# Convolution inputs and attention queries turned by way of DRAM, and the second half's groups dealt out anew, in a one-core hybrid block

## The chip, the cores and the metric

The kernel runs on one core of a Trainium2 chip. The metric is the device time of one launch in microseconds (us). One core has TensorE for matmuls (in the profile PE, and PEld for its weight loads), VectorE (DVE), ScalarE (ACT), GpSimd (POOL) and SyncE (SP), and 16 DMA engines that move data between the core's memory and DRAM. Matmul results go to PSUM, which here is cut into banks of 512 columns; all other tiles lie in SBUF.

## The reference

One layer of a streaming encoder on 256 tokens of 2048 features, all in float32:

```python
h = rms_norm(x, mix_norm)
proj = h @ w_in            # q|k|v|z|beta|alpha, mla_q|c_kv|k_rope, gate_a|gate_b
qkv = silu(causal_conv(concat([dn_q, dn_k, dn_v]), conv_w))     # 4 taps per channel
q_a, k_a = l2norm(q), l2norm(k);  o_a = gated_delta_rule(q_a, k_a, v_a, g, beta)   # 8 heads of 128
o_a = rms_norm(o_a) * silu(dn_z)
qn, qr = rms_norm(mla_q[:128]), rope(rms_norm(mla_q[128:]))     # 8 heads of 128 + 64
kn, v_b from rms_norm(c_kv) @ w_kv_up;  o_b = softmax attention, chunk-causal
y = sigmoid(gate_a) * (o_a @ w_branch_a) + sigmoid(gate_b) * (o_b @ w_branch_b)
x = x + y @ w_out
x = x + relu(rms_norm(x) @ w_mlp_up)^2 @ w_mlp_down
x = x + sigmoid(rms_norm(x) @ w_ple_gate) * (p @ w_ple)
```

The gated delta rule needs, per head and chunk, the inverse of a triangular matrix built from k, beta and the decays g, and then two recurrent steps.

## The kernel before

**Main stream.** All large matrix products run as one stream of *groups* (`stream`, from L411 on). A group is 512 (sometimes 464, 384 or 256) output columns of one product for all 256 tokens, accumulated in two PSUM banks over its rows of weights. It is cut into *steps* of 256 weight rows. In a step, `load` brings the weights from DRAM on SP's queue (tile `raw`, five buffers), `cut` splits them into a rounded high part `whi` on ACT and a remainder `wlo` on DVE (helper `split`, L260, recorded under L146; four buffers each, three steps ahead), and TensorE makes 12 matmuls: two rows of 128, two token blocks, and three products (high by high, high by low, low by high) at L501. Left operands are kept likewise as two parts, in `Acts` objects: `hT` (normed input), `cT` (the compressed latent), `obT` and `oaT` (outputs of the two branches), `yT`, `nT`, `uT`, `gT`.

**Groups' order.** The list `groups` gives it: first the small columns, the latent (`ckv`) and the queries of the attention (four groups `evac_mq` of two heads each, 384 columns, the first one inside the first group), with `kv0` to `kv3` (two steps each) among them; then six groups of convolution inputs, k, q, v of the first half of the heads and k, q, v of the second half (`evac_conv`); then four pairs of a gate group `gb` and a branch group on `obT` (`evac_bb`, four steps); then z, `ga`, the branch groups on `oaT`, and the rest. A step of kv, conv and gb groups takes the same 12 matmuls of 512 columns. Counting steps from zero, the first conv group begins at step 48, and the first `obT` group at step 104.

**Side work.** What lies between the products is written as generators that sit in four *lanes*: `L_MLA` (attention), `L_CONV`, `L_SOLVE` (delta rule) and `L_TURN`. After each step the planner `weave` is called twice; each call is one *tick* and runs one piece (up to the next `yield`) of one lane, at most every second tick for a lane. A lane runs its generators one after the other. A generator that waits yields False and costs no turn. Before a matmul of the main stream is written, `until` looks whether its left operand has been written by then; if not, it runs lanes without the gap, tick after tick, until it has. So the order in the program is settled when the program is built; a list scheduler then orders instructions on each engine by program order and by when it expects their inputs, so that an instruction whose inputs are late can be overtaken by later ones. ACT and DVE instructions that go through `keep_in_program_order` stay behind the one written before them on their engine.

**Transposes before.** The conv inputs come with tokens on partitions and must have channels there. `conv` does eight 128x128 transposes on TensorE (L895) into two PSUM banks, and ACT (first tap) and DVE (three taps) read the banks. After the SiLU, eight more TensorE transposes (L918) make token-major copies for norms, k and v. `evac_mq` norms and rotates the queries of two heads, transposes them on TensorE (L731 for the 128 plain, L732 for the 64 rotated features), and ACT and DVE bring the results to `qnT` and `qrT`.

**The way by DRAM that is there already.** Class `Carry` turns `oaT`, `yT`, `nT` and `gT`: DVE transposes 32x32 blocks (`turn`, L324), POOL's queue writes the tile to DRAM (L326) and fetches it back in four loads, one for 32 partitions each (L331); the pieces are read in the lane `L_TURN` 15 ticks after the fetch was written (`CARRY`).

**Gates' values.** `gates` makes the cumulated decays of 16 heads and token blocks (`gmid`, 128 partitions by 16) and writes them to DRAM transposed, element by element (L873); `decays` (L1257) reads them back as rows spread over all partitions.

**Delta rule.** `solve` waits until all four attention parts are done (`mla["ob"]`) and q, k and v of its half, then runs `inverse` and `recur`; the branch `oaT` needs both halves.

**Buffers.** `big` tiles (4 KB a partition) share 23 buffers, `mid` tiles (2 KB) 16; side work has four PSUM banks (`bank`), the main stream four (`acc`).

Of the kernel before, what the change touches and what calls it, by code (L numbers as in the profile page):

```python
# [9 lines left out]
F32 = mybir.dt.float32  # L10
# [7 lines left out]
P = 128  # L18
T = 256
# [133 lines left out]
def hybrid_block(ctx: ExitStack, tc: tile.TileContext, a, dbg=None):  # L153
# [14 lines left out]
    RAW_BUFS, SPLIT_BUFS, AHEAD, BIG_BUFS, EARLY, CARRY = 5, 4, 3, 23, 8, 15  # L168
# [146 lines left out]
    class Carry:  # L315
        def __init__(self, acts, k0):
            self.acts, self.k0, self.name = acts, k0, f"{acts.name}{k0}_"
            self.sq = big(f"sq_{self.name}", shape=(P, NT, 4, P))
            self.there = dpool.tile([NT, P, 4, P], F32, tag="there_sq", name=f"out_{self.name}")

        def turn(self, tb, src):

            tc.keep_in_program_order(
                nc.vector.transpose(self.sq[:, tb].rearrange("p j (k c) -> p k j c", k=4),  # L324
                                    src.rearrange("p (k j c) -> p k j c", k=4, j=4)))
            nc.gpsimd.dma_start(self.there[tb], self.sq[:, tb])  # L326

        def fetch(self, scales=None):
# [4 lines left out]
            return self.landed(land, scales, clock[0] + CARRY)  # L333
# [368 lines left out]

    def evac_mq(g, ps):
# [4 lines left out]
        def work():  # L708
# [19 lines left out]
            tn, tr = bank(f"tp_qn{g}"), bank(f"tp_qr{g}")  # L728
            for tb in range(NT):
                for e in range(2):  # L730
                    pe.transpose(tn[:, e * T + tb * P : e * T + (tb + 1) * P], q[:, tb, e, 0:HD], ident)  # L731
                    pe.transpose(tr[:ROPE, e * T + tb * P : e * T + (tb + 1) * P], rot[:, tb, e, :], ident)  # L732
            mla["qn"][g] = mid(f"qnT{g}")
            act.activation(mla["qn"][g], tn, AF.Copy, scale=gain("q_nope_norm"))
            mla["qr"][g] = mid(f"qrT{g}")
            nc.gpsimd.memset(mla["qr"][g][ROPE:, :], 0.0)
            dve.tensor_copy(mla["qr"][g][:ROPE, :], tr[:ROPE, :])
            yield
# [5 lines left out]
    def evac_kv(g, ps):  # L744
# [9 lines left out]
        def work():  # L754
# [16 lines left out]
            while not mla["kr"]:  # L771
                yield False
# [58 lines left out]
    gmid = cpool.tile([P, NT, NH], F32, name="gmid")  # L831
# [4 lines left out]
    def gates():  # L836
# [35 lines left out]
        with nc.allow_non_contiguous_dma(reason="small"):  # L872
            nc.gpsimd.dma_start(gmid_there.rearrange("b h p -> p b h"), gmid)  # L873
# [6 lines left out]
    def evac_conv(kind, half, ps):  # L880
# [3 lines left out]
        L_CONV.add(conv(kind, half, ev))  # L884

    def conv(kind, half, ev):

        yield
        acc = big(f"cv{kind}{half}", shape=(P, 4, T))
        for pair in range(2):  # L890
            tp = bank(f"tp_cv{kind}{half}{pair}").rearrange("p (h t) -> p h t", h=2)
            for e in range(2):
                for tb in range(NT):
                    h = 2 * pair + e
                    pe.transpose(tp[:, e, tb * P : (tb + 1) * P], ev[:, tb, h * P : (h + 1) * P], ident)  # L895
            for e in range(2):
                h = 2 * pair + e
                ct = "qkv".index(kind) * 8 + half * 4 + h
                w = lambda s: convw[:, (3 - s) * 24 + ct : (3 - s) * 24 + ct + 1]
                act.activation(acc[:, h, :], tp[:, e, :], AF.Copy, scale=w(0))  # L900
                for s in (1, 2, 3):
                    dve.scalar_tensor_tensor(acc[:, h, s:], tp[:, e, : T - s], w(s), acc[:, h, s:],
                                                   ALU.mult, ALU.add)
        yield
        y = acc
# [6 lines left out]
        if kind in "kv":  # L912
            tm = big(f"tm{kind}{half}", shape=(P, NT, 4, HD))
# [508 lines left out]
```

## Time and profile before

| | |
|---|---|
| time, median of three runs | 1529.3 us (1529.29 to 1529.53) |
| the profiled execution's own time | 1529.25 us |
| its span, first to last instruction | 1527.5 us |
| TensorE (PE) busy | 1517.3 us, 99% |
| VectorE (DVE) busy | 997.7 us, 65% |
| ScalarE (ACT) busy | 772.3 us, 51% |
| GpSimd (POOL) busy | 75.3 us, 5% |
| DMA, mean | 198 GB/s |

A row of the *timeline* has start, duration, engine, line, operation, written tile and read tiles, how many are merged, and in brackets the idle time ahead of it with what ended it. A row of one *tile's* view has shortest, median and longest duration in ns, the first and last start in us and the forms. A row of *windows* has the length of a stretch, busy time and number of instructions of PE, PEld, DVE, ACT and POOL, the granted clock, DMA share and GB/s. A row of *DMA issues* has the count, the size of each and the median time from issue to landing. The durations of matmuls overlap, since they are pipelined: their price is the distance of their starts.

### The profile page before, as it was taken

Reading aid. Unit: us, or ns where it says so; the run is one execution under the profiler, and the core shown is the slowest. Engines: PE = TensorE matmul, PEld = TensorE weight load, DVE = VectorE, ACT = ScalarE, POOL = GpSimd, SP = SyncE. Lnnn points to the kernel's source line nnn. Section 1 sums busy time; section 2 is a strip of 40 time slices with the busy share of each in tenths; the row PEclk is TensorE's granted clock in tenths of the full one; section 3 lists DMA queues with packets and bytes.
Section 4 is the critical chain, followed back from the end, with each engine's and each line's share of the span. In section 5 each row is a group of like instructions: output and inputs, shape, how many; then the busy total and the mean of one; then the engine's idle time right before and its main releaser. Section 6 shows DMA issues by size and latency. Waiting matters only on the chain.

```text
span 1527.5 us, 20738 instructions
## 1 busy us (share of the span) xinstructions
PE 1517.3 (99%) x7606; PEld 1291.4 (85%) x7606; DVE 997.7 (65%) x1755; ACT 772.3 (51%) x1182; POOL 75.3 (5%) x137
## 2 busy tenths in 40 slices
PE   9999999999999999999999999999999999999998
PEld 7898888888888888888888888888888888888888
DVE  7887687895686565866666565556554665456654
ACT  6665676644544444455454443344433453345643
POOL 0000000100100000211000000000000000001000
PEclk9999999999999999999999999999999999999999
DMA  8565444555365566987655555555555555567763
GB/s 311 145 207 181 152 152 154 181 191 197 122 205 187 167 217 210 287 298 238 214 189 190 193 192 193 193 190 187 191 193 193 192 200 193 193 220 239 230 201 117
DMA packets 94710, 301.83 MB, mean 198 GB/s; under 512 B 11088, under 2 KB 24272, under 8 KB 94608
## 3 DMA queue, kind: packets, MB, share of 16 engines
q1 hardware_dynamic: 87168, 281.61, 55.0%
q0 software_dynamic: 6576, 17.58, 4.3%
q8 instruction: 59, 0.97, 0.3%
q10 hardware_dynamic: 864, 1.32, 0.2%
q14 instruction: 43, 0.35, 0.1%
HBM read 290.50 MB, written 9.97 MB: 197 GB/s over the span
## 4 chain that ended last, share of the span: by engine, by line
PE 95%; DVE 2%; DMA 1%; ACT 1%; issue 0%; SPq 0%; DVEq 0%; ACTq 0%
PE ps L501 68%; PE ps L494 15%; PE ps L497 8%; DMA raw<-in_weights 1%; DVE wlo L146 1%; ACT whi L146 0%; PE tx L1081 0%; PE sc L785 0%; PE sc L786 0%; PE kk L979 0%; PE oo L1153 0%; PE kk L978 0%; PE vn L1136 0%; PE ov L821 0%; PE td L1089 0%
## 5 line engine op out<-in xcount | busy, mean ns | idle before, releaser
L146 DVE TENSOR_TENSOR wlo<-raw,whi 128x1024 fp32r<-128x1024 f32 (+3 forms) x541 | 643.6, 1192 | 461.4 <-ACT whi L146 458.9
L146 ACT CAST whi<-raw 128x1024 fp32r<-128x1024 f32 (+3 forms) x541 | 554.6, 1027 | 685.5 <-PE ps L501 453.0
L501 PE MATMUL ps<-whi,hT 128*128 128x512 f32 (+2 forms) x1344 | 415.7, 385 | 0.4 <-ACT whi L146 0.4
L501 PE MATMUL ps<-whi,uT 128*128 128x512 f32 x1024 | 315.7, 389 | 0.0
L501 PEld LDWEIGHTS ps<-whi,hT 128*128 128x128 f32 x1344 | 251.0, 188 | 44.6 <-ACT whi L146 1.4
L494 PE MATMUL ps<-nT,whi 128*128 128x512 f32 x1024 | 278.1, 393 | 0.0
L501 PE MATMUL ps<-wlo,hT 128*128 128x512 f32 (+2 forms) x672 | 256.7, 382 | 2.1 <-DVE wlo L146 2.1
L501 PEld LDWEIGHTS ps<-whi,uT 128*128 128x128 f32 x1024 | 192.3, 188 | 39.7
L501 PE MATMUL ps<-wlo,uT 128*128 128x512 f32 x512 | 199.2, 389 | 0.0
L494 PEld LDWEIGHTS ps<-nT,whi 128*128 128x128 f32 x1024 | 173.9, 188 | 22.9 <-DVE x L146 0.9
L497 PEld LDWEIGHTS ps<-nT,wlo 128*128 128x128 f32 x1024 | 155.5, 188 | 21.5
L497 PE MATMUL ps<-nT,wlo 128*128 128x256 f32 x1024 | 160.3, 278 | 0.0
L501 PEld LDWEIGHTS ps<-wlo,hT 128*128 128x128 f32 x672 | 126.3, 188 | 24.4 <-DVE wlo L146 3.8
L501 PEld LDWEIGHTS ps<-wlo,uT 128*128 128x128 f32 x512 | 96.1, 188 | 19.9
L501 PE MATMUL ps<-whi,gT 128*128 128x512 f32 (+1 forms) x312 | 80.9, 348 | 0.0
L501 PE MATMUL ps<-whi,yT 128*128 128x512 f32 x256 | 79.0, 389 | 0.0
L501 PEld LDWEIGHTS ps<-whi,gT 128*128 128x128 f32 x312 | 54.8, 189 | 7.6
L501 PEld LDWEIGHTS ps<-whi,yT 128*128 128x128 f32 x256 | 48.0, 188 | 10.1
L501 PE MATMUL ps<-wlo,gT 128*128 128x512 f32 (+1 forms) x156 | 54.3, 348 | 0.0
L501 PE MATMUL ps<-wlo,yT 128*128 128x512 f32 x128 | 49.8, 389 | 0.0
L501 PE MATMUL ps<-whi,obT 128*128 128x512 f32 x128 | 40.7, 391 | 0.0
L501 PE MATMUL ps<-whi,oaT 128*128 128x512 f32 x128 | 39.6, 389 | 0.0
(403 smaller groups left out, 1195.0 us busy)
## 6 DMA issues: line engine op xcount, KB each, us to landing
raw<-in_weights SPq DMA_DIRECT2D x492, 512.0 KB, 3.4
raw<-in_weights SPq DMA_DIRECT2D x24, 384.0 KB, 4.2
raw<-in_weights SPq DMA_DIRECT2D x16, 256.0 KB, 3.2
raw<-in_weights SPq DMA_DIRECT2D x7, 464.0 KB, 6.9
x<-in_x SPq DMA_DIRECT2D x4, 512.0 KB, 11.2
xT<-in_xT SPq DMA_DIRECT2D x7, 256.0 KB, 7.0
dt<-gmid_there POOLq DMA_DIRECT2D x4, 256.0 KB, 5.1
blk<-there POOLq DMA_DIRECT2D x8, 128.0 KB, 4.2
```

The lines of the kernel that those rows point to most:

```text
L146: i = f(*args, **kwargs)
L494: pe.matmul(ps[c], hi[:, j, cs], g.acts.both(k), start=first, stop=False)
L497: pe.matmul(ps[c][:, :T], lo[:, j, cs], g.acts.both(k)[:, :T], start=False, stop=last)
L501: pe.matmul(ps[tb], g.acts.at(k, part, tb), w[:, j, : g.n], start=(first and n_ == 0), stop=(last and n_ == 2),)
```

## The change

Four things are changed together.

1. A conv group's result goes by way of DRAM: a new generator `send` in `L_TURN` uses `Carry.turn` (two DVE transposes, two writes, four loads) and `conv` starts 15 ticks later, reads the landed tile in SBUF in place of PSUM, head by head with a yield after each, into an accumulator of its own (`acc`, with four columns of padding), and writes the SiLU over the landed tile. The eight transposes at L895 go away; those at L918 stay. Only the first token block's copy of k is still made.
2. The queries take the same way (`queries`, `queries_landed`): per pair of heads four DVE transposes, two writes, eight loads (four in pieces of 256 bytes, four in pieces of 128 bytes), and 15 ticks later (`QUERIES`) two ACT activations to `qnT`; the loads of the rotated features land in `qrT` itself. The transposes at L731 and L732 and DVE's copy go away. Attention now also waits for its queries at build time.
3. `gmid` is turned by one DVE transpose and written in four DMAs of rows of 128 bytes.
4. The groups' order: after k, q, v of the first half come `gb0` and its `obT` group, k of the second half, `gb1` and its group, q and v of the second half, and then the other two pairs. The first `obT` group now begins at step 80 in place of 104. `solve` starts with q (the group v comes last in a half, and only `recur` waits for it).

`big` tiles have 21 buffers in place of 23; two tiles of `inverse` and the copy of k move to `mid`.

```diff
+        def moved(self):
             land = big(f"land_{self.name}", shape=(P, 4 * NT, 4, 32))
             for j in range(4):
                 nc.gpsimd.dma_start(land[32 * j : 32 * j + 32].rearrange("p q k c -> p q (k c)"),
                                     self.there[:, :, j, :].rearrange("b (i r) x -> r (b i) x", i=4))
+            return land
...
+    def queries(g, q, rot):
+        sq = big(f"sq_q{g}", shape=(P, NT, 6, 64))
+        there = dpool.tile([NT, P, 6, 64], F32, tag="there_q", name=f"out_q{g}")
+        for tb in range(NT):
+            for c0, nj, src in ((0, 4, q[:, tb, :, 0:HD]), (4, 2, rot[:, tb])):
+                tc.keep_in_program_order(
+                    nc.vector.transpose(sq[:, tb, c0 : c0 + nj].rearrange("p j (e c) -> p e j c", e=2),
+                                        src.rearrange("p e (j c) -> p e j c", c=32)))
+            nc.gpsimd.dma_start(there[tb], sq[:, tb])
+        land, qr = mid(f"land_q{g}", shape=(P, 4 * NT, 2, 32)), mid(f"qrT{g}")
+        nc.gpsimd.memset(qr[ROPE:, :], 0.0)
+        for j in range(4):
+            nc.gpsimd.dma_start(land[32 * j : 32 * j + 32].rearrange("p q e c -> p q (e c)"),
+                                there[:, :, j, :].rearrange("b (i r) x -> r (b i) x", i=4))
+        for j in range(2):
+            for e in range(2):
+                nc.gpsimd.dma_start(qr[32 * j : 32 * j + 32, e * T : (e + 1) * T].rearrange("p (q c) -> p q c", c=32),
+                                    there[:, :, 4 + j, 32 * e : 32 * e + 32].rearrange("b (i r) c -> r (b i) c", i=4))
+        L_TURN.add(queries_landed(g, land, qr, clock[0] + QUERIES))
+        yield
...
-            tn, tr = bank(f"tp_qn{g}"), bank(f"tp_qr{g}")
-            for tb in range(NT):
-                for e in range(2):
-                    pe.transpose(tn[:, e * T + tb * P : e * T + (tb + 1) * P], q[:, tb, e, 0:HD], ident)
-                    pe.transpose(tr[:ROPE, e * T + tb * P : e * T + (tb + 1) * P], rot[:, tb, e, :], ident)
+            yield from queries(g, q, rot)
...
-        with nc.allow_non_contiguous_dma(reason="small"):
-            nc.gpsimd.dma_start(gmid_there.rearrange("b h p -> p b h"), gmid)
+        turned = mid("gmidT", shape=(P, 32))
+        dve.transpose(turned, gmid_room)
+        for i in range(4):
+            nc.gpsimd.dma_start(gmid_there.rearrange("b h p -> (b h) p")[:, 32 * i : 32 * i + 32],
+                                turned[32 * i : 32 * i + NT * NH, :])
...
+    def send(kind, half, ev):
+        yield
+        room = [mid(f"sq_cv{kind}1{tb}", shape=(P, 4, P)) for tb in range(NT)] if half else None
+        way = Carry(None, 0, f"cv{kind}{half}", room)
+        for tb in range(NT):
+            way.turn(tb, ev[:, tb, :])
+        L_CONV.add(conv(kind, half, way.moved(), clock[0] + CARRY))
+        yield
+    def conv(kind, half, land, due):
+        while clock[0] < due:
+            yield False
+        acc = mpool.tile([P, 4, T + 4], F32, tag="acc", name=f"cv{kind}{half}", bufs=2)
...
+        for h in range(4):
...
+            act.on = dve.on = True
+            act.activation(chunks(acc[:, h, 0:T]), land[:, :, h, :], AF.Copy, scale=w(0))
+            for s in (1, 2, 3):
+                out = chunks(acc[:, h, s : s + T])
+                dve.scalar_tensor_tensor(out, land[:, :, h, :], w(s), out, ALU.mult, ALU.add)
+            act.on = dve.on = False
+            yield
...
+    groups += [conv_group(kind, 0) for kind in "kqv"]
+    groups += branch(0)
+    groups.append(conv_group("k", 1))
+    groups += branch(1)
+    groups += [conv_group(kind, 1) for kind in "qv"]
+    for n in (2, 3):
+        groups += branch(n)
```

More of the change, by code (lines that the diff above doesn't have):

```diff
@@ L332, in fetch @@
                                     self.there[:, :, j, :].rearrange("b (i r) x -> r (b i) x", i=4))
-            return self.landed(land, scales, clock[0] + CARRY)
+            return land
+        def fetch(self, scales=None):
+            return self.landed(self.moved(), scales, clock[0] + CARRY)
         def landed(self, land, scales, due):
@@ L701, in squares_n, with queries_landed @@
         act.activation(junk[:, :n], src, AF.Square, accum_out=dst)
+    def queries(g, q, rot):
[18 more added lines that the diff above has]
+        yield
+    def queries_landed(g, land, qr, due):
+        while clock[0] < due:
+            yield False
+        qn = mid(f"qnT{g}")
+        for e in range(2):
+            tc.keep_in_program_order(
+                act.activation(qn[:, e * T : (e + 1) * T].rearrange("p (q c) -> p q c", c=32), land[:, :, e, :],
+                               AF.Copy, scale=gain("q_nope_norm")))
+        mla["qn"][g], mla["qr"][g] = qn, qr
+        yield
     def evac_mq(g, ps):
@@ L770, in work @@
             yield
-            while not mla["kr"]:
+            while not (mla["kr"] and mla["qn"][g] is not None):
                 yield False
@@ L883, in evac_conv @@
             act.activation(ev[:, tb, :], ps[tb], AF.Copy, scale=rxc[tb])
-        L_CONV.add(conv(kind, half, ev))
-    def conv(kind, half, ev):
+        L_TURN.add(send(kind, half, ev))
+    def send(kind, half, ev):
         yield
[L889 to L903, printed above, removed]
-        yield
-        y = acc
-        act.activation(y.rearrange("p a b -> p (a b)"), acc.rearrange("p a b -> p (a b)"), AF.Silu)
@@ L911, in conv @@
             g[kind + "T"] = y
-        if kind in "kv":
-            tm = big(f"tm{kind}{half}", shape=(P, NT, 4, HD))
+        if kind == "k":
+            g["k"] = mid(f"tmk{half}")
+        if kind == "v":
+            g["v"] = big(f"tmv{half}", shape=(P, NT, 4, HD))
         ss = small(8, f"l2{kind}")
@@ L1009, in inverse @@
         flip = big(f"flip{half}", shape=(P, BASE, BASE))
-        work = big(f"strip{half}", shape=(P, 2, STRIP, BASE))
+        work = mid(f"strip{half}", shape=(P, 2, STRIP, BASE))
         sol, prod = work[:, 0], work[:, 1]
@@ L1016, in inverse @@
         act.copy(sol[:, :, 0:1], unit[:, :, 0:1])
-        for _ in range(5):
+        for _ in range(7):
             yield
@@ L1140, in recur @@
                 kd = mid(f"kd{half}")
-                dve.tensor_tensor(v4(kd), k[:, 0], per_head(heads(eto, 0, half)), ALU.mult)
+                dve.tensor_tensor(v4(kd), v4(k), per_head(heads(eto, 0, half)), ALU.mult)
             yield
@@ L1263, in solve @@
             decays(0)
-        while mla["ob"] < 4 or not all(c in gdn[half] for c in ("qT", "kT", "k", "v", "rq")):
+        while mla["ob"] < 4 or not all(c in gdn[half] for c in (("made", "k"), ("made", "q"))):
             yield False
@@ L1268, in solve, with evac_q @@
             decays(1)
+        while ("made", "v") not in gdn[half]:
+            yield False
         yield from recur(half)
-    def evac_v(half, ps):
-        evac_conv("v", half, ps)
+    def evac_q(half, ps):
+        evac_conv("q", half, ps)
         L_SOLVE.add(solve(half))
```

56 lines of the change are left out of this document (30 added, 26 removed).

## The prediction

> **What bounds the kernel now.** I read the page first, then windows for where TensorE (PE) is idle, then the timeline of PE around single side pieces. The first line below is the page's first part; the others are rows of the windows (length; busy time of PE, PEld, DVE, ACT, POOL; clock; DMA share; GB/s).
>
> ```profile
> PE 1517.3 (99%) x7606; PEld 1291.4 (85%) x7606; DVE 997.7 (65%) x1755; ACT 772.3 (51%) x1182; POOL 75.3 (5%) x137
> ...
> 57.00:76.00 19.00, 17.54 (x98) 16.28 (x96) 13.18 (x60) 11.40 (x21) 2.77 (x4) 1.00 0.67 126
> 76.00:130.00 54.00, 52.70 (x283) 48.07 (x283) 47.75 (x176) 35.81 (x90) 0.00 (x0) 1.00 0.64 206
> 130.00:270.00 140.00, 139.35 (x703) 117.33 (x702) 102.16 (x243) 95.40 (x202) 1.64 (x3) 1.00 0.46 156
> 270.00:530.00 260.00, 260.00 (x1325) 220.21 (x1324) 188.91 (x387) 125.83 (x176) 24.11 (x44) 1.00 0.54 177
> ```
>
> PE is busy throughout at full clock (1.00). In the region that the change touches, 57 to 530 us, it is idle 1.46 + 1.30 + 0.65 + 0 = 3.4 us. So an instruction taken off PE there shortens the end by its own price, and a new wait lengthens it; work added to DVE (102 of 140 us) or ACT (95 of 140) costs nothing as long as PE's inputs keep coming. Nothing after 530 us is changed.
>
> **Conv transposes: -5.3 us.** The timeline of PE around one conv's eight, and the tile's row of the v groups:
>
> ```profile
> 274.95 1.03 PE L895 MATMUL tp_cvq<-cst,evq 128*128 128x128 f32 x8
> 275.74 0.48 PE L501 MATMUL ps<-whi,hT 128*128 128x512 f32 x1
> 276.06 0.40 PE L501 MATMUL ps<-wlo,hT 128*128 128x512 f32 x1
> 276.29 0.62 PE L501 MATMUL ps<-whi,hT 128*128 128x512 f32 x2
> ...
> L895 PE MATMUL tp_cvv<-cst,evv x16: 270/272/273, 214.4 to 299.3; 128*128 128x128 f32 x16
> ```
>
> The eight push the main stream back by 275.74 - 274.95 = 0.79 us, and the next distance is 0.32 instead of 0.23: 0.88 us in all. Sixteen for v are two convs; k and q run the same code, so six convs, 6 x 0.88 = 5.3 us. DVE gets 12 block transposes at 0.65 us each (a row two parts below), 7.8 us spread over 130 us with DVE 27% free: hidden.
>
> **Query transposes: -2.6 us, not -3.5.** Each of the four pieces has eight as well (four of 128 features, four of 64).
>
> ```profile
> L731 PE MATMUL tp_qn<-cst,mq x16: 271/272/273, 63.2 to 166.8; 128*128 128x128 f32 x16
> ...
> 88.15 0.27 PE L731 MATMUL tp_qn<-cst,mq 128*128 128x128 f32 x1
> ...
> 90.25 0.34 PE L501 MATMUL ps<-whi,hT 128*128 128x384 f32 x1
> 91.58 0.96 PE L501 MATMUL ps<-whi,cT 128*128 128x512 f32 x3 [0.99 <-DVE cT L146]
> ```
>
> At 0.88 us that is 3.5. But the second piece's run while PE waits for `cT` anyhow (0.99 us idle remain at 91.58): taking these away only widens the wait. I count three pieces, 2.6 us; the bound is 3.5. The scheduler has put one matmul of a later group (128x384, at 90.25) ahead of the waiting ones; that row comes back below.
>
> **Gates' values: -1.0 us.** One DMA of 8 KB in 4-byte elements; its issue row, and windows:
>
> ```profile
> gmid_there<-gmid POOLq DMA_DIRECT2D x1, 8.0 KB, 14.3
> ...
> 68.00:69.00 1.00, 1.00 (x8) 1.00 (x7) 0.00 (x0) 0.00 (x0) 0.00 (x0) 1.00 0.24 15
> 71.00:72.00 1.00, 1.00 (x8) 0.91 (x6) 0.00 (x0) 0.23 (x1) 0.00 (x0) 1.00 1.05 372
> 72.00:76.00 4.00, 3.02 (x15) 2.23 (x13) 3.33 (x10) 3.94 (x11) 0.00 (x0) 1.00 0.87 312
> ```
>
> While it is under way all traffic falls to 15 GB/s, ACT and DVE have no weights to split, and from 72 to 76 us PE is idle 0.98 us. Rows of 128 bytes should end that: -1.0 us (bounds 0, if another cause holds the weights, and -1.5, all idle time of 57 to 76).
>
> **New waits on moved data: 0 us.** Turn, write and fetch of the branch output that goes this way already, with the median landing of the slowest fetch, and pieces of 128 bytes as the delta rule fetches them:
>
> ```profile
> 546.39 1.30 DVE L324 STREAM_TRANSPOSE sq_oaT__5632<-o 128x512 f32<-128x512 f32 x2
> ...
> 547.39 1.15 POOL L326 DMA_DIRECT2D out_oaT__5633<-sq_oaT__5632  x2 [16.77 <-DVE sq_oaT__5632 L324]
> 551.38 2.35 POOL L331 DMA_DIRECT2D land_oaT__5678<-out_oaT__5633  x4 [2.83 <-DMA out_oaT__5633<-sq_oaT__5632]
> ...
> land_yT__6293<-out_yT__6284 POOLq DMA_DIRECT2D x4, 128.0 KB, 8.4
> ...
> tr<-back POOLq DMA_DIRECT2D x4, 64.0 KB, 4.0
> ```
>
> From 546.4 to the last landing: 551.38 + 2.35 + 8.4 - 546.39 = 15.7 us at the slowest. The pieces are read 15 ticks, 7.5 steps, later: 7.5 x 12 x 0.23 = 20.7 us. Queries have eight fetches, 2.35 us more, 18.1 us, and some steps are narrower (384 columns, some 0.17 us a matmul): about 18 us, no margin. What is queued behind the waiting ACT activation is the split of the weights; those are cut three steps ahead, so a lateness under two steps (4 to 5 us) reaches no matmul. POOL's fetches wait for the writes and hold up the next piece's write, but pieces come some 14 us apart or more, except k's and the fourth query pair's (five ticks), whose fetch still ends in time by the same sum. I take 0; bound +2. Buffers: `big` falls to 21; counting live tiles I find at most one write (`o`) that waits a step, off PE's path.
>
> **The groups' order: +3.5 us.** This is the step with the widest bounds. The last of four attention parts writes `obT` at 264.9 us, the first `obT` group begins at 319 us:
>
> ```profile
> L501 PE MATMUL ps<-whi,obT x128: 388/389/478, 319.3 to 445.5; 128*128 128x512 f32 x128
> ...
> L146 DVE TENSOR_TENSOR obT<-ov,obT x4: 683/685/692, 150.1 to 264.9; 128x512 fp32r<-128x512 f32 x4
> ```
>
> Step 104 is at 319.3 us, and (319.3 - 264.9) over 2.76 us a step (12 x 0.23) puts the last part near step 84 or 85. The attention lane goes one piece every two ticks before and after, and has as many pieces; counting its turns for the new order I get the same step. But now `bb0` stands at steps 80 to 83, and its last step, 83, needs that part. So `until` must write the rest (transposes of k, scores, softmax, product) without gaps: I count 13 forced ticks. What that rest takes, by the timeline of the fourth part:
>
> ```profile
> 243.54 0.60 PE L767 MATMUL tp_kn<-cst,kn 128*128 128x128 f32 x4
> 244.59 0.69 ACT L146 ACTIVATE knT<-tp_kn,par 128x512 f32<-128x512 f32 x1
> 246.75 0.38 PE L785 MATMUL sc<-knT,qnT 128*128 128x128 f32 x2
> 248.94 0.59 PE L786 MATMUL sc<-krT,qrT 128*128 128x256 f32 x2
> 252.44 0.69 DVE L146 TENSOR_REDUCE smx<-sc 128x2 f32<-128x512 f32 x1
> 256.63 0.48 ACT L146 ACTIVATE pr<-sc,snm 128x256 f32<-128x256 f32 x1
> 257.44 0.62 DVE L146 TENSOR_SCALAR pr<-pr,srs 128x256 f32<-128x256 f32 x2
> 258.46 0.38 PE L814 MATMUL ptA<-cst,pr 128*128 128x128 f32 x2
> 259.00 0.27 PE L815 MATMUL ptB<-cst,pr 128*128 128x128 f32 x1
> 260.68 0.64 ACT L146 COPY pt<-ptA 128x512 f32<-128x512 f32 x1
> 261.87 0.59 PE L821 MATMUL ov<-pt,vb 128*128 128x256 f32 x2
> 262.95 0.38 PE L822 MATMUL ov<-pt,vb 128*128 128x128 f32 x2
> 263.80 0.67 ACT L146 CAST obT<-ov 128x512 fp32r<-128x512 f32 x1
> ```
>
> Without the gaps: 0.60 + 0.69 + scores 2.78 (246.75 to 249.53) + 0.69 + four exponentials 1.9 + 0.62 + 0.81 + 0.64 + product 1.46 + 0.67 + 0.69 = 11.5 us; as it ran, 243.5 to 265.6, 22 us. PE itself works 5.65 us of it (work that it has before and after). The rest can be covered: three steps of the next group (`k` of the second half, whose left operand is there) have their weights cut, 3 x 2.76 = 8.3 us, if the scheduler lets them overtake as at 90.25. Lower bound: 11.5 - 5.65 - 8.3 < 0, no stall. Upper bound: 22 - 5.65 = 16.4 us, nothing overtakes. The nearest row is the wait for `cT`: from 88.15 to 91.58, 3.4 us, PE was idle 0.99, 29%. 29% of 11.5 is 3.4; I take 3.5.
>
> **Sum.** -5.3 - 2.6 - 1.0 + 3.5 = -5.4 us on the profiled execution's 1529.25 us (span 1527.5 and 1.75 around it; the median, 1529.3, is the same to 0.05): **1523.8 us**.
>
> **Rivals.** (a) *The wait is hidden altogether*: the scheduler fills it. 1529.25 - 8.9 = 1520.3. For it: three cut steps, and no idle time at all in 270 to 530 us, where the delta rule's side pieces also hang on each other. Against: those pieces stand two ticks apart, these do not. (b) *Slower*: nothing overtakes, and PE stands for the whole chain at the pace at which it ran: 1529.25 - 8.9 + 16.4 = 1536.8. It gets slower at all once the stall passes 8.9 us. For it: ACT and DVE must also do the conv of v, the norms of q and table loads in those ticks; against: the overtaking row. The Trainium skill (TensorE: Matmul & The Clock Gate, "Why this matters for your kernels") warns of PE-idle gaps of more than about 3 us, after which the clock halves for a while; the longest idle time here is 0.99 us with the clock at 1.00, so no row shows it, and it would come on top of this case. (c) *Forced ticks load ACT and DVE*: the conv of v comes with them, and its twelve DVE operations, pinned in program order, go ahead of the next weights' remainders:
>
> ```profile
> L146 DVE SCALAR_TENSOR_TENSOR cvv<-tp_cvv,par,cvv 128x255 f32<-128x255 f32 x8 | 3.5, 476 | 0.0
> ```
>
> At 3.5 / 8 = 0.44 us that is 5.3 us more: 1523.8 + 5.3 = 1529.1, no change. (d) *Small pieces hold up the weights as the gates' values did*: each query move fetches 1,024 pieces of 256 bytes and 1,024 of 128. If each of four moves cost the 0.98 us above: 1523.8 + 3.9 = 1527.7. Against: `tr`, in pieces of 128 bytes, lands in 4.0 us, and PE is never idle around it (270 to 530). By the Trainium skill (DMA: Bandwidth & Descriptors, "Specifications") transfers under 512 bytes fall below line rate because of a read-modify-write; that speaks for (d), and the row of `gmid` agrees with it at 4 bytes, the row of `tr` hardly does at 128.
>
> **How the numbers follow.** The forecast (stall between 1 and 6 us, own range 1521 to 1526) 0.37; (a) 0.28; (b) 0.13; (c) 0.10; (d) 0.12. The range for 8 in 10 leaves out (b) and a gain beyond all bounds: the low end is all gains at their bounds without a stall, -5.3 - 3.5 - 1.5, and the 0.65 us of idle time in 130 to 270 us, 1518.3; the high end takes in (d), and (c) with a stall of 6 us in place of 3.5, to 1531.6. A measurement of this kernel tells 0.2%, 3.1 us, from no change: faster below 1526.2 is the forecast and (a), 0.65; within is (c) and (d), 0.22; slower, above 1532.4, is (b), 0.13.
>
> **What would show it.** No L895, L731 and L732; some 9 us less of PE's side work before 320 us; no stretch at 15 GB/s after `gmid`. The wait: PE idle behind ACT or DVE `obT`, shortly after 230 us, with matmuls of `hT` of the second half's k group ahead of the last `obT` ones. The moved data: no ACT wait for `land`. I am wrong if that idle time is over 6 us or under 1, if PE waits for `whi` or `wlo` there for longer than for `obT`, or if TensorE waits where the queries are used.

## The result, and the profile after

The changed kernel takes **1518.5 us** (median; 1518.2 to 1519.4) beside 1529.3 us before: a ratio of 0.9929, 95% interval 0.9919 to 0.9939, or 10.8 us less. Its profiled execution took 1518.87 us, with a span of 1517.1 us where the kernel before had 1527.5. So 10.4 us of span are to be explained.

First the changed kernel's page (busy time of the engines), then rows of its windows (length; busy time of PE, PEld, DVE, ACT, POOL; clock; DMA share; GB/s):

```profile
PE 1508.3 (99%) x7526; PEld 1283.2 (85%) x7526; DVE 1002.3 (66%) x1780; ACT 775.9 (51%) x1186; POOL 120.4 (8%) x223
```

```profile
57.00:76.00 19.00, 18.37 (x107) 17.99 (x107) 17.49 (x85) 15.57 (x34) 2.10 (x4) 1.00 0.62 193
76.00:130.00 54.00, 53.11 (x280) 48.43 (x279) 48.81 (x189) 38.28 (x99) 18.35 (x32) 1.00 0.79 242
130.00:270.00 140.00, 139.95 (x684) 117.11 (x683) 101.87 (x227) 86.12 (x163) 23.19 (x44) 1.00 0.58 190
270.00:530.00 260.00, 259.95 (x1308) 219.44 (x1308) 192.91 (x402) 138.22 (x208) 26.41 (x49) 1.00 0.58 189
```

PE has 80 instructions fewer (48 conv and 32 query transposes) and is busy 1517.3 - 1508.3 = 9.0 us less, 0.11 us each. In 57 to 530 us it is idle 0.63 + 0.89 + 0.05 + 0.05 = 1.6 us, before 3.4: 1.8 us less. Outside of this stretch single executions differ by some tenths. The clock is 1.00 throughout. What PE still waits for, by the view of waits (us in total, times, longest):

```profile
PE ps L505 <- DVE wlo L146: 1.5, 3, 0.7
...
PE ps L505 <- ACT cT L146: 0.9, 1, 0.9
```

The row left out between the two is a wait at PE's start-up (1.4 us, as before). Of the 1.5 us for `wlo` 0.63 lie in this stretch, at 64.7 us; the rest is ahead of 11 us. There is no wait for `obT`, and none for landed data. What became of the wait that the new order was to bring, after 230 us? The timeline of PE in the changed kernel, from the fourth attention part's transposes of k to the last `obT` step, 83:

```profile
238.21 0.60 PE L794 MATMUL tp_kn<-cst,kn 128*128 128x128 f32 x4
238.57 0.48 PE L505 MATMUL ps<-whi,hT 128*128 128x512 f32 x1
...
249.55 0.70 PE L848 MATMUL ov<-pt,vb 128*128 128x256 f32 x2
249.90 0.58 PE L505 MATMUL ps<-wlo,hT 128*128 128x512 f32 x1
...
253.04 0.38 PE L849 MATMUL ov<-pt,vb 128*128 128x128 f32 x2
253.18 0.70 PE L505 MATMUL ps<-whi,hT 128*128 128x512 f32 x2
...
254.19 0.40 PE L505 MATMUL ps<-whi,obT 128*128 128x512 f32 x1
```

The chain runs from 238.2 to 254.2 us, 16 us, and wherever PE would wait for it there stand matmuls on `hT` of the next groups: 45 of them by the matmul records, 45 x 0.227 = 10.2 us. With the chain's own matmuls (5.65 us by the prediction's count) that is all of the 16 us. The scheduler let nearly four steps overtake, not three.

The moved pieces land 4 to 5.5 us after their issue, soon enough for PE not to wait, by the view of DMA issues (count, size of each, median us to landing):

```profile
land_q<-out_q POOLq DMA_DIRECT2D x16, 64.0 KB, 4.5
land_cvk<-out_cvk POOLq DMA_DIRECT2D x8, 128.0 KB, 5.4
```

### The profile page after: what moved, and what is told of

Its sections match the earlier page's. It is cut to its first block, busy times and chain, and to the rows that moved or that the text cites. A ratio compares the mean times of both kernels' runs of the same rounds, so it can differ in the third digit from the quotient of the medians.

```text
span 1517.1 us, 20785 instructions
## 1 busy us (share of the span) xinstructions
PE 1508.3 (99%) x7526; PEld 1283.2 (85%) x7526; DVE 1002.3 (66%) x1780; ACT 775.9 (51%) x1186; POOL 120.4 (8%) x223
## 4 chain that ended last, share of the span: by engine, by line
PE 97%; DVE 1%; ACT 1%; DMA 0%; issue 0%; SPq 0%; DVEq 0%
PE ps L505 70%; PE ps L498 16%; PE ps L501 8%; PE tx L1122 0%; DMA raw<-in_weights 0%; DVE wlo L146 0%; PE sc L812 0%; PE sc L813 0%; PE vn L1177 0%; PE ov L848 0%; PE kk L1020 0%; ACT whi L146 0%; PE oo L1194 0%; PE kk L1019 0%; PE td L1130 0%
```

## The experiments

All are compared with the kernel before on the same chip; on these chips that one takes 1530.8 to 1531.0 us, so ratios are used, and differences in us are ratios times 1530.8.

### The groups' order

**The old order, with the rest of the change.**

```diff
-    groups += [conv_group(kind, 0) for kind in "kqv"]
-    groups += branch(0)
-    groups.append(conv_group("k", 1))
-    groups += branch(1)
-    groups += [conv_group(kind, 1) for kind in "qv"]
-    for n in (2, 3):
+    for half in range(2):
+        groups += [conv_group(kind, half) for kind in "kqv"]
+    for n in range(4):
         groups += branch(n)
```

> The changed kernel with the groups in the order of before (six conv groups, then four pairs of gb and obT group); everything moved as in the change. Theory 'cover' (the forced wait costs nothing, since later matmuls fill it): the old order takes no forced wait away that cost anything, but by my count of ticks the delta rule now ends nine steps later, and its output is fetched with 2 and 6 forced ticks at the first branch group on oaT (steps 192 and 194), where a fetch of 12 to 16 us has no matmuls of a later group with a ready operand before it but two steps each of the next branch groups: 1518.5 + 0 to 4 us, 1518.5 to 1522.5, with PE idle behind oaT or land. Rival 'stall' (the prediction's 3.5 us for the order): 1515.0, faster by 3.5 us. Rival 'order is nothing': 1518.0 to 1519.0.

Measured: 1523.4 us, ratio 0.9951 (0.9935 to 0.9968), 7.5 us less than before. The changed kernel has 0.9923 (0.9908 to 0.9939), measured on another chip (below). The intervals just touch, but all times here are 1523.0 us and more and there 1519.3 and less, beside equal times of the kernel before. So beside the old order the new one does not cost time, it *gains* some 4 us. The profile shows where. Windows and then the timeline of PE with the old order:

```profile
580.00:582.00 2.00, 0.15 (x1) 0.15 (x2) 0.58 (x1) 2.00 (x4) 0.00 (x0) 1.00 1.00 332
582.00:584.00 2.00, 2.00 (x6) 1.33 (x7) 2.00 (x5) 1.00 (x3) 0.00 (x0) 0.66 0.44 115
584.00:586.00 2.00, 2.00 (x6) 1.52 (x6) 0.23 (x1) 0.00 (x0) 0.00 (x0) 0.50 0.61 225
586.00:588.00 2.00, 2.00 (x10) 1.63 (x9) 0.32 (x1) 1.05 (x1) 0.00 (x0) 0.99 0.00 0
```

```profile
581.85 0.50 PE L505 MATMUL ps<-whi,oaT 128*128 128x512 f32 x1 [2.12 <-ACT oaT L146]
```

PE waits 2.1 us for `oaT`, and then its clock is halved, from 582.6 to 586.0 us by windows of 0.1 us (6 matmuls in the two us from 584, 10 in the next two). That makes 2.1 + 3.4 / 2 = 3.8 us; another 0.5 us of idle time lies in 270 to 530 us. One timeline row each, of the old order's kernel and of the changed one, shows why: the fetch of `oaT`'s first half.

```profile
563.93 2.34 POOL L332 DMA_DIRECT2D land_oaT__5785<-out_oaT__5738  x4 [3.83 <-DMA out_oaT__5738<-sq_oaT__5737]
```

```profile
541.62 2.34 POOL L332 DMA_DIRECT2D land_oaT__5636<-out_oaT__5589  x4 [3.38 <-DMA out_oaT__5589<-sq_oaT__5588]
```

With the old order it starts 22 us later, and the step that needs `oaT` (PE's row above) waits for the splitting of what lands. With the new one the early `obT` step forces the attention's pieces forward, and the delta rule, which by the code waits for attention, starts earlier: the last part of `obT` is written at 254.1 us in place of 271.2, the delta rule's first matmuls (`kk`) start at 257.8 in place of 274.4, and the product `o` of its second half at 513.9 in place of 535.7. No run moved the delta rule by itself. Nor is the late start all of it: the first half's `o` is ready at 459.3 us with the old order (462.2 with the new), and yet its block transposes for the way to DRAM come at 558.0 (536.1), behind the second half's product. With the convolutions alone (below) the second half's product comes just as late, at 535.9 us, but the first half's block transposes follow at 536.5 and PE does not wait for `oaT`. What holds them back was not looked into.

**The overtaking taken away.** The first half of the matmuls of step 84, the first behind the last `obT` step of `bb0`, stays in program order:

```diff
-                            pe.matmul(
+                            mm = pe.matmul(
                                 ps[tb], g.acts.at(k, part, tb), w[:, j, : g.n],
                                 start=(first and n_ == 0), stop=(last and n_ == 2),
                             )
+                            if i == 84 and j == 0:
+                                tc.keep_in_program_order(mm)
```

> The changed kernel, in which the matmuls of the first half of step 84 (the first step of the second half's k group) are kept in program order on PE, behind the last obT matmuls of bb0, so that no matmul of the next group can overtake the wait. In the changed kernel 45 matmuls of that group ran before the last 12 of bb0, 45 x 0.227 = 10.2 us. Theory 'cover': PE stands idle for them, less what the part gains when ACT and DVE have no more weights to split: 6 to 10 us, 1524.5 to 1528.5, idle time behind sc, pr, pt, ov and obT. Rival 'stall' (the wait was paid already or is short): 1518.5 to 1520.5. If the clock falls after a gap of over 3 us, as the Trainium skill (TensorE: Matmul & The Clock Gate) has it, the matmuls after it are further apart than 0.23 us for a while and the time is 1 to 4 us longer still.

Measured: 1531.6 us, ratio 1.0004 (0.9995 to 1.0013): the whole gain of the change is gone, some 12 us (6 to 10 were expected, and 1 to 4 more if the clock fell). Windows of this kernel, and PE's timeline in the chain:

```profile
245.00:250.00 5.00, 2.88 (x8) 1.30 (x7) 4.90 (x23) 2.29 (x7) 0.00 (x0) 0.58 0.00 2
250.00:255.00 5.00, 2.53 (x8) 2.06 (x9) 2.06 (x8) 2.81 (x3) 0.11 (x1) 0.50 0.00 0
...
130.00:270.00 140.00, 132.59 (x630) 110.18 (x629) 96.76 (x223) 81.43 (x159) 20.78 (x39) 0.95 0.56 176
```

```profile
244.81 0.30 PE L843 MATMUL ptA<-cst,pr 128*128 128x128 f32 x1 [1.89 <-DVE l2y L146]
...
251.20 0.80 PE L851 MATMUL ov<-pt,vb 128*128 128x128 f32 x2 [1.82 <-DVE pt L146]
```

140 - 132.59 = 7.4 us idle, and PE's busy time is 5.5 us more than in the changed kernel (1513.8 by its page, against 1508.3). The clock explains 4.9 of these: it is at half from 245.8 to 259.5 us, and PE is busy for 9.8 us in there. The price of an uncovered chain is real; overtaking is what pays it.

### The gates' values

**In rows, alone in the kernel before.**

```diff
-        with nc.allow_non_contiguous_dma(reason="small"):
-            nc.gpsimd.dma_start(gmid_there.rearrange("b h p -> p b h"), gmid)
+        turned = mid("gmidT", shape=(P, 32))
+        dve.transpose(turned, gmid_room)
+        for i in range(4):
+            nc.gpsimd.dma_start(gmid_there.rearrange("b h p -> (b h) p")[:, 32 * i : 32 * i + 32],
+                                turned[32 * i : 32 * i + NT * NH, :])
```

> The kernel before with the gates' values in rows of 128 bytes (one DVE transpose, four DMAs), nothing else. Theory 'gates hold up the weights': 1529.3 - 1.0 = 1528.3, as low as 1527.5. Rival: 1529.0 to 1529.6, the idle time of PE from 57 to 76 us stays at 1.46 us.

Measured: 1527.1 us, ratio 0.9977 (0.9967 to 0.9986), 3.5 us less, twice the most that was expected. The issue row of the new writes (it was 14.3 us to landing before), and windows of this kernel:

```profile
gmid_there<-gmidT POOLq DMA_DIRECT2D x4, 2.0 KB, 2.6
...
68.00:69.00 1.00, 1.00 (x8) 1.00 (x7) 1.00 (x5) 0.60 (x2) 0.00 (x0) 1.00 1.12 310
57.00:76.00 19.00, 18.48 (x108) 18.11 (x108) 17.45 (x85) 15.64 (x34) 3.55 (x7) 1.00 0.61 183
76.00:130.00 54.00, 53.86 (x290) 49.15 (x290) 46.23 (x166) 34.56 (x81) 0.00 (x0) 1.00 0.65 197
```

At 68 us the traffic is 310 GB/s, where it was 15, and DVE works for all of that microsecond, where it stood still. Idle time of PE: 0.52 + 0.14 us. The kernel before, on a chip of the experiments, has 2.09 + 1.24 (rows below). So 2.7 us are shown: the weights behind the write, and also the wait for `cT`, since DVE is no longer behind with the weights' remainders. The other 0.8 us aren't placed; ahead of 57 us, where the edit does nothing yet, single executions differ by as much (idle 2.0 us in this one; 3.0 in the kernel before on this occasion, 2.2 in its first profile).

**In 4-byte elements, in the changed kernel** (the same lines the other way round).

> The changed kernel with the gates' values written to DRAM element by element, in one DMA, as before. Theory 'gates hold up the weights': the prediction's 1.0 us comes back, up to 1.8 with the idle time that fell elsewhere: 1519.5 to 1520.3, with windows under 50 GB/s between 59 and 70 us. Rival 'the weights were late for another cause': 1518.0 to 1518.9.

Measured: 1525.7 us, ratio 0.9967 (0.9955 to 0.9979): undoing it costs 6.7 us, more than doing it gained alone, and far more than the 1.8 expected at most. Windows and PE's timeline of this kernel:

```profile
57.00:76.00 19.00, 17.09 (x96) 16.13 (x97) 12.85 (x68) 11.08 (x19) 1.29 (x1) 1.00 0.65 121
76.00:130.00 54.00, 50.63 (x252) 45.79 (x251) 45.94 (x174) 37.62 (x104) 14.13 (x25) 0.94 0.79 234
...
94.00:96.00 2.00, 2.00 (x7) 1.52 (x6) 0.35 (x1) 0.00 (x0) 0.63 (x2) 0.50 0.97 235
96.00:98.00 2.00, 2.00 (x6) 1.61 (x5) 0.09 (x1) 0.95 (x3) 0.00 (x0) 0.50 0.73 188
```

```profile
89.53 0.50 PE L505 MATMUL ps<-whi,cT 128*128 128x512 f32 x1 [0.89 <-ACT cT L146]
...
93.23 1.65 PE L505 MATMUL ps<-whi,cT 128*128 128x512 f32 x3 [2.34 <-DVE cT L146]
```

Idle time grows by 1.28 us in 57 to 76 and by 2.48 us in 76 to 130, and the clock stands at half from 91.9 us, still inside the long wait, to 98.7 us. PE is busy for 5.45 us of that, which costs 2.7 us: 1.28 + 2.48 + 2.7 = 6.5 us, nearly all of the 6.7.

Why is the wait for `cT` so much longer than the 0.99 us of the kernel before? DVE's rows, first of the kernel before, then of this one:

```profile
72.63 0.96 DVE L146 TENSOR_TENSOR wlo<-raw,whi 128x768 fp32r<-128x768 f32 x1 [5.78 <-ACT whi L146]
...
91.05 0.87 DVE L146 SCALAR_TENSOR_TENSOR cT<-tp_cT__1080,par,cT 128x256 fp32r<-128x256 f32 x2
```

```profile
73.72 0.96 DVE L146 TENSOR_TENSOR wlo<-raw,whi 128x768 fp32r<-128x768 f32 x1 [6.11 <-ACT whi L146]
...
92.70 0.87 DVE L146 SCALAR_TENSOR_TENSOR cT<-tp_cT__1085,par,cT 128x256 fp32r<-128x256 f32 x2
```

While the slow write is under way DVE has no weights to split and stands still for some 6 us. From then on it works with one pause of 0.55 us until it begins `cT`'s remainders, 18.4 us later in the kernel before and 19.0 us later here. So in this stretch DVE sets when the product that needs the remainders can start, and side work of PE ahead of that product costs nothing. The queries' transposes of the first two pieces (at 78.2 and 88.2 us in the kernel before) lie there. Without the first eight PE comes to `cT` 0.8 us sooner, measured from DVE's restart; where the second eight stood it now waits 0.89 us for ACT; and DVE is 0.6 us later, as four block transposes of a piece take it 1.1 us and the copy that they replace took 0.6. Together that is 2.2 us, the step from 0.99 to 0.89 + 2.34 us.

**Is it the clock?** Eight matmuls on finished operands, whose result is not used, put into that wait:

```diff
+            if i == 32:
+                fill = bank("fill")
+                for _ in range(8):
+                    tc.keep_in_program_order(
+                        pe.matmul(fill, hT.at(0, 0, 0), hT.both(0), start=True, stop=True))
```

> The changed kernel with the gates' values written in 4-byte elements, and with 8 matmuls of 128x512 (0.23 us each) that compute nothing put on TensorE where it waits 2.34 us for cT; their output is not read. Theory (the clock): the gap shrinks to about 0.5 us, the granted clock stays at 0.99 or more between 92 and 100 us, and the kernel is 2 to 3 us faster than the one with 4-byte elements alone (ratio to before 0.995 instead of 0.9967), though it does more work. Rival (the wait itself costs the time, the clock nothing): the same time as the one with 4-byte elements (0.9967), or up to 1.8 us more where the fillers hold up the matmuls behind them (0.998).

Measured: 1525.1 us, ratio 0.9964 (0.9952 to 0.9977): not told apart from the kernel without them (0.9967). The timeline shows that I had misplaced them: they fill the first wait (0.89 us, for ACT), and the second is as before:

```profile
93.60 1.03 PE L510 MATMUL ps<-whi,cT 128*128 128x512 f32 x2 [2.27 <-DVE cT L146]
...
97.35 0.62 PE L510 MATMUL ps<-whi,cT 128*128 128x512 f32 x2
```

It still tells something: after nearly the same gap, with PE busy ahead of it, the clock is at half from 93.8 to 97.3 us only (two matmuls in 0.46 us again; 0.85 us at half clock), 3.4 us in place of 6.8. Then, ten of them at the right place:

```diff
                         for n_, (part, w) in enumerate(((0, hi), (0, lo), (1, hi))):
+                            if i == 32 and j == 0 and tb == 0 and n_ == 2:
+                                fill = bank("fill")
+                                for _ in range(10):
+                                    tc.keep_in_program_order(
+                                        pe.matmul(fill, hT.at(0, 0, 0), hT.both(0), start=True, stop=True))
                             pe.matmul(
```

> The changed kernel with 4-byte gates' values and 10 matmuls of 128x512 that compute nothing, put this time behind the second product with cT, where the 2.3 us wait for the low part from VectorE stands; the 0.9 us wait ahead of the first product stays. Theory (TensorE's clock falls where enough idle time falls together): idle time there falls from 2.3 to about 0.1 us, the clock stays at 0.99 or more from 92 to 100 us, and the kernel is about 2.6 us faster than the one with 4-byte elements alone, ratio to before 0.995. Rival: the low clock is no result of the gap (but of what runs then), stays at 0.50 for about 5 us, and the time is the 0.9967 of the one without these matmuls.

Measured: 1524.8 us, ratio 0.9961 (0.9948 to 0.9975). Windows and timeline of this kernel:

```profile
94.00:96.00 2.00, 2.00 (x10) 1.64 (x10) 1.93 (x17) 0.15 (x1) 0.23 (x1) 1.00 1.03 242
96.00:98.00 2.00, 2.00 (x11) 1.65 (x10) 2.00 (x12) 0.69 (x1) 0.00 (x0) 1.00 0.88 210
```

```profile
90.12 2.47 PE L509 MATMUL fill<-hT 128*128 128x512 f32 x10
93.25 0.73 PE L510 MATMUL ps<-whi,cT 128*128 128x512 f32 x2 [0.67 <-DVE cT L146]
```

The third product with `cT` begins at 93.25 us as it did at 93.23, but the clock stays at 1.00, and 21 matmuls are made from 94 to 98 us in place of 13. In these executions useless work in the gap kept the clock, and it is worth 2.0 us (span 1522.6, against 1524.6). In the timed executions the difference is 0.9 us and the intervals overlap, so the 2.6 us that I expected are not shown. The mean clock of each execution goes with this: without the ten matmuls it is 0.997 in two of six executions (1526.4 and 1526.7 us), 0.998 in one (1525.9) and 0.999 in three (1525.2 to 1525.4); with them it is 0.999 or 1.000 in all five (1524.4 to 1525.4). So without them the clock does not stay low equally long in every execution, and the profiled one was among the two with the lowest clock.

### Queries and convolutions

**The queries alone in the kernel before** (part 2 of the change).

```diff
-            tn, tr = bank(f"tp_qn{g}"), bank(f"tp_qr{g}")
...
+            yield from queries(g, q, rot)
...
-            while not mla["kr"]:
+            while not (mla["kr"] and mla["qn"][g] is not None):
```

> The kernel before with the attention's queries by way of DRAM, nothing else (gates' values in 4-byte elements, old order, 23 big tiles). As predicted, three pieces count and the second one's time goes into the wait for cT: 1529.3 - 2.6 = 1526.7. Rival 'all four count' (DVE and ACT are freed too, and the wait for cT shrinks): 1525.5 to 1526.0. Rival 'small pieces hold up the weights' (0.98 us a move): 1530.6.

Measured: 1531.9 us, ratio 1.0007 (0.9997 to 1.0017): 32 transposes less, and no gain. The view of waits of this kernel, and a window:

```profile
PE ps L501 <- DVE cT L146: 2.4, 1, 2.4
```

```profile
94.00:96.00 2.00, 2.00 (x6) 1.57 (x5) 0.59 (x2) 0.00 (x0) 1.02 (x2) 0.50 0.95 276
```

It is the wait of the 4-byte experiment again, with the slow write at its root: the transposes of the first two pieces had lain in the stretch in which DVE sets the time of that product. Beside the kernel before on the chips of the experiments, PE is idle for 2.2 us more in 57 to 530 us, and the half clock (92.2 to 99.0 us, PE busy for 5.57 of them) costs 2.8 us; less the 3.5 us of 32 transposes that is +1.5, where +1.1 was measured.

**Queries and rows together**, still without the convolutions and the new order (both edits above):

```diff
+            yield from queries(g, q, rot)
...
+        turned = mid("gmidT", shape=(P, 32))
+        dve.transpose(turned, gmid_room)
```

> The kernel before with the gates' values in rows and the queries through DRAM, convolutions and order of groups as before. Alone the rows were worth 3.7 us and the queries cost 1.0 us. Theory (the queries lost time only because the wait for cT, which the slow write of the gates' values causes, was no longer filled): with the rows there the queries gain 2.6 to 3.5 us more, 6.3 to 7.2 us in all (ratio 0.9953 to 0.9959). Rival (the queries' way through DRAM costs time of its own): the two add up, 2.7 us (ratio 0.998).

Measured: 1525.5 us, ratio 0.9964 (0.9951 to 0.9976), 5.5 us less. That lies between the two: more than adding up gives, less than 6.3. The trace has the reason, a new wait at another place:

```profile
295.18 0.33 PE L923 MATMUL tp_cvv<-cst,evv 128*128 128x128 f32 x1 [1.76 <-ACT evv L146]
```

```profile
294.00:296.00 2.00, 0.57 (x3) 0.38 (x4) 0.71 (x4) 2.00 (x4) 0.00 (x0) 1.00 0.02 8
296.00:298.00 2.00, 2.00 (x14) 1.74 (x13) 1.33 (x2) 2.00 (x4) 0.00 (x0) 1.00 0.00 0
```

A conv's transposes on PE wait 2.0 us for their input (1.76 and 0.25 more within the eight); in the kernel before they start 1.8 us after it is there, and in the changed kernel there are none. On ACT that input stands behind `flip`, a step of the delta rule's inverse that waited 3.47 us for its own fetch (at 292.6 us). Without those 2.0 us the queries would be worth some 4 us on top of the rows' 3.5, a little above the 2.6 to 3.5 of the theory; that is argued, since the wait was not taken away by itself. The clock did *not* fall here.

**The convolutions alone in the kernel before** (part 1, `solve` beginning with q, 21 buffers; old order):

```diff
+        L_CONV.add(conv(kind, half, way.moved(), clock[0] + CARRY))
...
-    RAW_BUFS, SPLIT_BUFS, AHEAD, BIG_BUFS, EARLY, CARRY = 5, 4, 3, 23, 8, 15
+    RAW_BUFS, SPLIT_BUFS, AHEAD, BIG_BUFS, EARLY, CARRY = 5, 4, 3, 21, 8, 15
```

> The kernel before with the conv groups' inputs by way of DRAM and the smaller changes that go with it (solve starting with q, 21 big tiles, two tiles in mid), in the old order of groups, queries on PE and gates' values as before. By the transposes alone: 1529.3 - 5.3 = 1524.0. If the later delta rule exposes the fetch of oaT in the old order: 1524 to 1528, with PE idle behind oaT or land near the branch groups on oaT. Rival 'more than the transposes' (PSUM banks and ACT and DVE freed): 1523.0 to 1523.7.

Measured: 1525.1 us, ratio 0.9964 (0.9951 to 0.9977), 5.5 us less, beside the 5.3 of the forecast. The agreement is partly luck, for the clock fell here too, behind the slow write of the gates' values (75.1 to 78.5 us). A window of this kernel:

```profile
76.00:78.00 2.00, 2.00 (x8) 2.00 (x8) 1.97 (x4) 1.92 (x9) 0.00 (x0) 0.50 0.74 236
```

Beside the kernel before on these chips, PE's busy time is 3.75 us less (1514.3 against 1518.05): 48 x 0.11 = 5.3, of which 3.4 us at half clock take 1.7 back. The rest of the gain is idle time, 1.8 us less in 57 to 530 us; while the clock is low DVE catches up, and the wait for `cT` goes.

This kernel has no wait for `oaT`; with the old order that came only once the queries' way and the rows were there too.

The parts alone add up to -3.5 + 1.1 - 5.5 = -7.9 us, the three together without the order give -7.5, and the order 4.3 more, with the old order's wait for `oaT` gone.

### Both kernels again, on the chips of the experiments

No edit in either.

> The kernel before, unchanged, for its profile on the chip of the experiments, where it takes about 1530.9 us, and 1529.3 us on the first. If the 1.6 us more are a gap of TensorE that grew over the length at which the clock falls, the profile shows a granted clock under 0.9 in some slice between 57 and 130 us where the first profile shows 0.99 or more, and idle time of TensorE about the same. If they are spread over the whole program, the clock is as before and no stretch is longer than in the first profile by more than 0.5 us.

> The changed kernel, unchanged, beside the kernel before on the chip of the experiments. First run: 1518.5 against 1529.3 us. If the disturbed stretch of the kernel before alone differs between chips, the changed kernel stays at 1518 to 1519 us and is 12 to 12.5 us shorter than the kernel before; if the chip is slower as a whole, it takes about 1520 us, and the difference stays at 10.8 us.

Measured: before 1531.4 us (1530.8 in the runs beside it), after 1519.0; ratio 0.9923 (0.9908 to 0.9939). Windows of the kernel before, here:

```profile
0.00:57.00 57.00, 53.96 (x242) 45.79 (x243) 43.80 (x113) 39.35 (x77) 1.08 (x7) 1.00 0.75 255
57.00:76.00 19.00, 16.91 (x97) 15.97 (x97) 12.56 (x72) 10.78 (x17) 2.77 (x4) 1.00 0.67 109
76.00:130.00 54.00, 52.76 (x284) 48.16 (x284) 47.75 (x174) 37.04 (x97) 0.00 (x0) 1.00 0.67 210
```

Neither expectation for the kernel before holds: the clock is 1.00, but there are 0.8 us more idle time ahead of 57 us, and 0.63 more in 57 to 76 (2.09, against 1.46 in the first profile), where it waits for weights behind the slow write. The changed kernel has 0.64 us there on this chip and 0.63 on the first, so for these two executions the difference is gone.

### A version without the wait for `cT`

The largest wait that the changed kernel has left in the stretch that was changed is 0.9 us for `cT`. The groups of keys and values are put behind the queries':

```diff
+    for g in range(1, 4):
+        groups.append(Group(hT, w_in, C_MQ + 384 * g, 384, KD, bind(evac_mq, g)))
     for g in range(4):
-        if g:
-            groups.append(Group(hT, w_in, C_MQ + 384 * g, 384, KD, bind(evac_mq, g)))
-        if g > 1:
-            groups.append(Group(cT, wkv, 512 * (g - 2), 512, 4, bind(evac_kv, g - 2)))
-    for g in (2, 3):
```

> The changed kernel with the four groups of keys and values behind the four groups of queries, instead of in between: the first product with cT then stands 12 steps later. If the 0.9 us for which TensorE waits for cT is the last that this start has to give, that wait goes, nothing takes its place, and the kernel is 0.9 us faster than the changed kernel (ratio to before 0.9917 beside 0.9923). Rival: attention's second half starts later, its forced work of 8 ticks and the delta rule's oaT come late, and TensorE waits 1 to 3 us between 230 and 260 us or at 570 to 590 us: ratio 0.993 to 0.995.

Measured: 1518.0 us (1517.9 to 1518.1), ratio 0.9915 (0.9902 to 0.9929), beside the changed kernel's 1518.8 to 1519.3 on a chip where the kernel before takes the same. A window of this kernel:

```profile
76.00:130.00 54.00, 54.00 (x280) 49.28 (x279) 50.25 (x188) 37.62 (x99) 18.93 (x33) 1.00 0.85 249
```

No idle time is left in 76 to 130 us, 0.89 us less; 0.4 us come back at 244 us (a wait for `l2y` on DVE). The 0.9 us expected are near the difference of the times, but the intervals of the ratios overlap, and the trace shows only 0.5 us net, so no more than that is shown.

## Why the prediction was right, and where it was wrong

It said faster, 1523.8 us in 1518.3 to 1531.6; it is 1518.5, close to the low end, and nearest to rival (a), 1520.3. The direction and the range held. The stall of 3.5 us, which the forecast rested on, did not come, and by the prediction's own sign it is wrong there: idle time behind `obT` under 1 us. Step by step:

- **PE bounds the kernel, an instruction off it shortens the end by its price**: right in the end, as busy time fell by 9.0 us and the span by 10.4; but only because no cover was lost. The queries alone took 32 instructions off PE and gained nothing.
- **Conv transposes, -5.3**: right in size, at 0.11 us each. That they gave 5.5 alone is partly luck, as shown above.
- **Queries, -2.6 and not -3.5**: the choice failed, the bound held. I took only the second piece's transposes to be free, by the wait for `cT`. With the slow write DVE, from 72.6 us on, sets when that wait ends, so the first piece's are free as well and DVE's added work costs; the share of DVE's free time that I used (27%) is an average over 130 to 270 us and says nothing of that stretch. With the rows of the gates' values DVE begins `cT`'s remainders at 87.7 us in place of 91.0, PE waits for ACT alone (0.9 us), and all four pieces count: 80 transposes off PE gave 9.0 us, where 5.3 + 3.5 is 8.8. The two terms are not independent, and the sum treated them so.
- **Gates' values, -1.0**: by the first two profiles the idle time in 57 to 130 us fell by 1.2 us, so the term was near as a row of that sum. As a cause it was undersized: 3.5 us alone, and 6.7 if undone. I had seen only the weights' wait at 72 to 76 us, not that DVE, too, is late from there on (`cT`'s remainders begin at 92.7 us where it is undone), nor the clock.
- **New waits on moved data, 0**: right in the changed kernel, with landings of 4 to 5.5 us and no wait of PE. With the old order it would not have held: `oaT` then came 2.1 us late.
- **The groups' order, +3.5**: the step that failed. The forced step came as counted, and the chain took 16 us, between my 11.5 and 22. The share of 29% left over, taken from the wait for `cT`, had no ground (29% of 11.5 is also 3.3, not 3.4): there few matmuls could overtake, here 45 did, and nothing was left over. The lower bound (no stall) was what my own row of three cut steps gave. And I priced the order as a loss only. Beside the kernel before it is worth nothing, but it takes away a wait for `oaT`, some 4 us with its clock, that the other parts bring with the old order; I had priced that wait at nothing.
- **A term that was missing**: 0.6 us of wait for `kn` in 130 to 270 us goes away. I had it in the low end only.

With these sizes the sum is -5.3 - 3.5 - 1.2 - 0.6 + 0 = -10.6 us, beside 10.4 of span.

The rivals: (a) is what happened to the wait. (b) is a true mechanism: with overtaking taken away, the chain costs some 12 us, 7.4 idle and some 5 by the clock, where I had 16.4 us. The Trainium skill (TensorE: Matmul & The Clock Gate, "Why this matters for your kernels") warns of PE-idle gaps of more than about 3 us, after which the clock halves. The halving came, but without a gap of that length: three gaps of 0.93, 1.89 and 1.05 us between 239 and 246.2 us were enough. (c) did come, and was covered as the rest was: on DVE's timeline of the changed kernel seven operations of the conv of v stand ahead of the copy that the product waits for.

```profile
248.95 2.85 DVE L146 SCALAR_TENSOR_TENSOR cvv<-land_cvv,par,cvv 128x256 f32<-128x256 f32 x7
...
251.72 0.42 DVE L146 COPY pt<-ptB 128x256 f32<-128x256 f32 x1
```

(d) didn't come: PE waits 0.63 us for `wlo` in the changed stretch, where the kernel before waits 1.2 us for `wlo` and 0.4 for `whi`.

The time therefore doesn't depend on the chain's length, as the prediction had it, but on whether the scheduler has matmuls to put ahead.

## What to carry to other kernels

Before side work is taken off the engine that sets the time, look whether it fills a wait: if it does, remove the wait's cause in the same change, or the gain turns into idle time. Price a forced wait by the independent work that the scheduler may put ahead of it, counted instruction by instruction, not by a share taken from another place. Ask of each stretch which engine sets its time: an average over a longer one hides it. And test parts together as well as alone: here one alone gained nothing and was worth its full price with the others.

## What was not expected of the hardware

The granted clock falls to half after gaps that look harmless, and it stays there for whole multiples of one length. By windows of 0.1 us it is at half for 3.4 us with the old order (from 582.6 us), with the eight misplaced matmuls (from 93.8) and with the convolutions alone (from 75.1); for 6.8 us with the 4-byte elements (from 91.9) and with the queries alone (from 92.2); and for 13.65 us with the overtaking taken away (from 245.8). That is once, twice and four times 3.41 us. In the 3.41 us ahead of each fall PE was busy for 0.8 to 1.85 us.

The length of a gap does not decide alone. With the convolutions alone gaps of 1.00 and 0.56 us, 0.4 us apart, were enough; the kernel before has 1.07 and 0.55 us at the same place on the chips of the experiments, and the clock stayed at 1.00, as it did after 1.76 + 0.25 us at 293 us.

The Trainium skill (TensorE: Matmul & The Clock Gate, "What's actually happening") says that activity is judged in a free-running window of about 3.4 us. The multiples of 3.41 us agree with such a window, and so does the fact that like gaps end differently. That a whole window must be idle isn't borne out, since PE was busy for at least 0.8 us ahead of each fall. Where the windows begin in an execution that keeps its clock can't be read from its profile, so how much work would have been enough stays open.
